# Activation transposes moved from TensorE to VectorE blocks and DMA, with a reordered product schedule, in a one-core hybrid decoder layer

## The chip, the cores and the metric

One NeuronCore of a Trainium2 chip runs the whole layer in one launch. The metric is the device time of that launch in microseconds (us). Five engines work side by side: TensorE (PE in the profile, with its weight loads as PEld), VectorE (DVE), ScalarE (ACT), GpSimd (POOL) and SyncE (SP), which here issues every DMA, the transfers between HBM and SBUF or within SBUF, in program order.

## The reference

The layer takes 256 tokens of width 2048 in float32 and computes

    h = rmsnorm(x);  y = h @ w_in                       # 2048 x 5120
    mix = [differential attention(q, k, v), conv module(u)] @ w_out
    x = x + rmsnorm(mix)
    h = rmsnorm(x)                                      # the second norm
    f = (silu(h @ w_gate) * (h @ w_up)) @ w_down        # D_FF = 5632
    x = x + rmsnorm(f)

The change touches the last three lines: the feed-forward half, and the end of the norm that feeds it.

## The kernel before

Every weight is used in float32 accuracy from two reduced-precision pieces. A weight tile of 512 x 512 (1 MB) is loaded by SP into a tile `w` (three buffers), or, for some tiles, into `raw`; ACT copies it rounded into `wh` (L185, L922), DVE subtracts to get the rest `wl` (L186, L923). PE then does, for each half of the tokens (`tb`, 128 of them), 12 matmuls of 128 x 512: four with high operand times `wh`, four with low operand times `wh`, interleaved, then four with high operand times `wl`. These 12 are called a step here. `wh` and `wl` have four buffers each, so tile i+4 can be split once PE is done with tile i.

D_FF is cut into 11 columns of 512, f = 0 to 10, in four parts (0 to 2, 3 to 5, 6 to 8, 9 and 10). Column 0 is done plainly. Each other column is a `Pair`: gate and up share products of a Strassen-like scheme. Seven products P1 to P7 take one step each, the gate tiles g0, g1 and the up tiles u0, u1 two steps each; 15 steps in all with the up tiles of the column before (the `fill`) placed inside. The order is P1, u0 (of the column before, or down tiles of the part before), P7, P6, u1, P5, P2, P3, g0, g1, P4. Four subtractions of whole tiles (L956) make the weights of later products; `last_sum` is one of them. P7 goes into PSUM bank b7, the products P1, P6, P5, P3 accumulate in bank b1. After P5, ACT copies b1 to a tile `s` and DVE adds b7 (L1025, L1026); P3 cannot write b1 before that copy.

After u1, DVE forms the activation `sg` (L1014, L1035): 128 tokens by 512 columns for each tb. `act_put` turns it round for the down product: PE transposes eight 128 x 128 blocks into PSUM (L1044; L845 for column 0), ACT rounds them into the high piece of the tile `act` (L208) and DVE makes the low piece (L209).

When the columns of a part are done, the down product runs for four column groups n = 0 to 3, each over the two or three `act` tiles of the part, two steps a tile. In the last part the loads of the norm's gain `gpf` and of `xres` (3 MB together, `reload`) are queued after the split of the first down tile.

The order of work on every engine is the order of the Python program. A list of steps is walked; before each step the side jobs that are due run (`yield n` means: go on n steps later), then the split of the tile four places ahead of the one just finished, with the loads that this lets go (`pump`) and its `post` subtractions. So whatever a job issues stands in each engine's queue ahead of what later steps issue. `needs` makes a down step wait in the program for its `act_put`.

`residual(1)` ends the first half for the second 128 tokens: transposes, then the sums of H2 tiles for the scheme (`form_sums`, `split_sums`), four squares (ACT), and the norm factor `rffn` that the first gate waits for.

Pools that matter here: T has 13 tiles of 1 MB, M has three of 512 KB.

Of the kernel before, what the change touches and what calls it, by code (L numbers as in the profile page):

```python
# [31 lines left out]
P = 128  # L32
# [12 lines left out]
C = 512  # L45
# [15 lines left out]
def hybrid_layer_kernel(ctx: ExitStack, tc: tile.TileContext, x, xt, pack, lamv,  # L61
# [635 lines left out]
    def square_into(src, acc):  # L697
        j = M("junk")
        nc.scalar.activation(j[:, :C], src, ACTF.Square, accum_out=acc)
# [26 lines left out]
    def form_sums():  # L726

        r = v3(T("sums"), 4)
        h, l = H2.part(1)
        for tb in range(2):  # L730
            tok = slice(tb * P, (tb + 1) * P)

            nc.vector.tensor_tensor(out=r[:, 2 * tb:2 * tb + 2].rearrange("p a (k t) -> p (a k) t", k=4),
                                    in0=h[:, :, tok].bitcast(F32), in1=l[:, :, tok].bitcast(F32),
                                    op=ALU.add)
        for o, a, b, op in [(3, 2, 3, ALU.add), (2, 0, 2, ALU.subtract), (0, 3, 0, ALU.subtract),
                            (1, 1, 0, ALU.subtract)]:
            nc.vector.tensor_tensor(out=r[:, o], in0=r[:, a], in1=r[:, b], op=op)
        return r
# [7 lines left out]
    def residual(tb, bank):  # L747
        xr, mg = st_["x", tb], st_["mixg", tb]
        tok = slice(tb * P, (tb + 1) * P)
        square_into(bank, part[:, tb, 3:4])  # L750
        if tb:
            yield 1
        nc.vector.tensor_tensor(out=mg[:, 3 * C:], in0=bank, in1=st_["gpost"][:, 3 * C:],
                                op=ALU.mult)
        r = partial_rstd(part, tb, "rpost")

        def x2(n):
            c = slice(n * C, (n + 1) * C)
            nc.vector.scalar_tensor_tensor(out=xr[:, c], in0=mg[:, c], scalar=r[:, 0:1],
                                           in1=xr[:, c], op0=ALU.mult, op1=ALU.add)  # L760

        def tr(n):
            bk = aux_bank("ht")
            for j in range(4):
                nc.tensor.transpose(bk[:, j * P:(j + 1) * P],
                                    xr[:, n * C + j * P:n * C + (j + 1) * P], ident)
            for eng in range(2):
                for j in range(4):
                    k = n * 4 + j
                    g = pk[:, PK_GFFN + k:PK_GFFN + k + 1]  # L770
                    h, l = H2.at(k, 1, tok)
                    b = bk[:, j * P:(j + 1) * P]
                    if eng == 0:
                        nc.scalar.activation(h[:, 0], b, ACTF.Copy, scale=g)
                    else:
                        nc.vector.scalar_tensor_tensor(out=l[:, 0], in0=b, scalar=g,
                                                       in1=h[:, 0].bitcast(F32), op0=ALU.mult,
                                                       op1=ALU.subtract)

        x2(0)  # L780
        yield 1
        x2(1)
        x2(2)
        yield 1
        x2(3)
        tr(0)
        for n in range(1, 4):
            yield 1
            tr(n)
        if tb:  # L790
            yield 1
            r = form_sums()
            yield 1
            split_sums(r)
        else:
            yield 3
        for n in range(4):
            square_into(xr[:, n * C:(n + 1) * C], part2[:, tb, n:n + 1])
        yield 1
        rstd2[tb] = partial_rstd(part2, tb, "rffn")  # L800

        nc.sync.dma_start(xd[tb], xr)
        st_["x", tb] = None

    oc = []
    need = {0: [lambda: st_["av", 0]], 4: [lambda: st_["av", 1]],
# [26 lines left out]
    def post_up(f, A, k, bank):  # L833
        while ("gate", f) not in st_:
            yield 1
        sg = st_["sg", f]
        for tb in range(2):
            nc.vector.scalar_tensor_tensor(out=sg[:, tb], in0=bank[tb], scalar=rstd2[tb][:, 0:1],
                                           in1=sg[:, tb], op0=ALU.mult, op1=ALU.mult)
            dve[0] += 0.6  # L840
        yield 2
        for tb in range(2):
            bk = aux_bank("ft")
            for j in range(4):
                nc.tensor.transpose(bk[:, j * P:(j + 1) * P], sg[:, tb, j * P:(j + 1) * P], ident)  # L845
            A.put_psum(k, 4, slice(tb * P, (tb + 1) * P), v3(bk, 4))

    def down_evac(pi, last, n, tb, bank):
        c = slice(n * C, (n + 1) * C)
# [39 lines left out]
    class Act:  # L889
# [9 lines left out]
            t = self.t[f]  # L899
            return t[:, 0, k % 4:k % 4 + n, tok], t[:, 1, k % 4:k % 4 + n, tok]  # L900

        put_psum = Operand.put_psum

    class Slot:

# [22 lines left out]
    class Pair:  # L928
# [5 lines left out]
        def __init__(self, f, A, k, last):  # L934
            self.f, self.A, self.k, self.last = f, A, k, last
            cols = [(f * C, C)]
            gt = [WTile(w_gate, 4 * i * P, SPLIT, cols) for i in range(4)]
            ut = [WTile(w_up, 4 * i * P, SPLIT, cols) for i in range(4)]
            self.g, self.u = gt[:2], ut[:2]
            self.r11, self.r21, self.r12, self.r22 = gt[2], gt[3], ut[2], ut[3]  # L940
            self.x = Slot()
            p = self.p = {
                1: Product(self, 1, self.r11, None, [("w", self.r11)]),
                7: Product(self, 7, self.r12, "r", [("r", self.r12), ("r", self.r22)]),
                6: Product(self, 6, self.x),
                5: Product(self, 5, self.r11, "w", [("w", self.x)]),
                2: Product(self, 2, self.r21, None, [("r", self.r21)]),
                3: Product(self, 3, self.r22, "r"),
                4: Product(self, 4, self.x, "w")}

            p[1].post = [lambda: self.sub(self.r11, self.r12, self.r11)]
            p[7].post = [lambda: self.sub(self.x, self.r22, self.r11)]
            p[3].post = [self.last_sum]

        def sub(self, out, a, b):
            nc.vector.tensor_tensor(out=out.w, in0=a.w, in1=b.w, op=ALU.subtract)  # L956
# [5 lines left out]
        def steps(self, fill):  # L962

            fill[0][0][1].post = [lambda: self.sub(self.r12, self.r22, self.r12)]
            s = {n: [(self, t, n, 0)] for n, t in self.p.items()}
            g = [[(self, t, f"g{i}", tb) for tb in range(2)] for i, t in enumerate(self.g)]
            return (s[1] + fill[0] + s[7] + s[6] + fill[1] + s[5] + s[2] + s[3] + g[0] + g[1] + s[4])

        def up_steps(self):
            return [[(self, t, f"u{i}", tb) for tb in range(2)] for i, t in enumerate(self.u)]  # L970
# [46 lines left out]
        def after(self, what, tb):  # L1017
            if what == 1:
                self.v = v3(M("v"), 2)
                nc.scalar.copy(self.v[:, 0], self.b1)  # L1020
            elif what == 6:
                nc.scalar.copy(self.v[:, 1], self.b1)
            elif what == 5:
                self.s = M("s")[:, :C]
                nc.scalar.copy(self.s, self.b1)  # L1025
                nc.vector.tensor_tensor(out=self.s, in0=self.b7, in1=self.s, op=ALU.add)  # L1026
            elif what == "g1" and tb == 0:
                self.sg = v3(M("sg"), 2)
                spawn(self.gate(0, self.b2, self.v[:, 0])).run()
            elif what == 4:  # L1030
                spawn(self.gate(1, self.b7, self.v[:, 1])).run()
            elif what == "u1" and tb == 0:
                self.up(0, self.b1)
            elif what == "u1":
                nc.vector.tensor_tensor(out=self.s, in0=self.b8, in1=self.s, op=ALU.add)  # L1035
                self.up(1, self.s)
                st_["act", self.f] = spawn(act_put(self.A, self.k, self.sg),
                                             1 if self.last else 3)

    def act_put(A, k, sg):  # L1040
        for tb in range(2):
            bk = aux_bank("ft")
            for j in range(4):
                nc.tensor.transpose(bk[:, j * P:(j + 1) * P], sg[:, tb, j * P:(j + 1) * P], ident)  # L1044
            A.put_psum(k, 4, slice(tb * P, (tb + 1) * P), v3(bk, 4))
        yield 1

    def reload():
        load_gain(1, "gpf")
# [6 lines left out]
    for pi, (f0, f1) in enumerate(parts):  # L1056
# [25 lines left out]
        for n in range(4):  # L1082
            c = Chunk("down", A, needs=needs)
            ts = w_tiles(w_down, f0 * C, [(n * C, C)], 0, nk)
            if last and n == 0:
                ts[0][1].post.append(reload)
            if last and n == 3:
                c.done = lambda tb, c=c, pi=pi: spawn(finish(pi, tb, c.bank[tb]))
                add(c, ts, stagger=True)
                continue  # L1090
            both(lambda bank, pi=pi, last=last, n=n: post_down(pi, last, n, bank))(c)
            st = steps_of(c, ts)
            if n == 3:
                put(st[:-4])
                fill = [st[-4:-2], st[-2:]]
            else:
                put(st)
# [82 lines left out]
```

## Time and profile before

| what | us |
|---|---|
| median of 3 runs | 1071.24 (1070.83 to 1071.37) |
| the profiled execution | 1072.81 |
| its span, first to last instruction | 1071.0 |
| PE busy in it | 1049.2 |
| DVE busy | 822.8 |
| ACT busy | 562.0 |

The mean granted TensorE clock is 0.997 of full speed. The span is 1.8 us shorter than the profiled execution's time, which also holds the launch around it. A busy PE in this profile includes the pipeline's own overlap, so the spacing of matmul starts says more than the busy share.

### The profile page before, as it was taken

To read this page: it belongs to the slowest core of one execution; us is meant where nothing else is said; L and a number is where in the kernel's file an instruction comes from. 1 tells how busy PE (TensorE), PEld (TensorE's weight loads), DVE (VectorE), ACT (ScalarE), POOL (GpSimd) and SP (SyncE) were. 2 spreads that over 40 slices of the span, in tenths; PEclk is the share of its full clock that TensorE was granted. 3 is DMA by queue.
4 is the path that set the end of the run, shared out by engine and by line. 5 is a ranking of instruction groups with operands and counts; after the bars stand their busy time and mean duration, and the time that the engine had idled before them with its cause. 6 is when DMAs were issued, how large, how long until landed. Compare 5 with 4: busy or idle time off the path is not lost.

```text
span 1071.0 us, 12013 instructions
## 1 busy us (share of the span) xinstructions
PE 1049.2 (98%) x4766; PEld 863.2 (81%) x4766; DVE 822.8 (77%) x858; ACT 562.0 (52%) x586; POOL 10.8 (1%) x16
## 2 busy tenths in 40 slices
PE   9999999999999989999999999999999999999996
PEld 7778788787888768878888887888888788888885
DVE  6589989898655779875568988557898865788765
ACT  6764664665644656564354756334465643446541
POOL 0000000001000000000000000000000000000000
PEclk9999999999999999999999999999999999999999
DMA  9876555545656638276454636854653776272852
GB/s 307 290 272 204 175 180 169 185 135 180 239 198 234 198 113 305 88 269 243 156 196 158 242 121 232 294 171 129 225 184 131 242 283 220 79 277 79 317 193 79
DMA packets 114264, 213.97 MB, mean 200 GB/s; under 512 B 4088, under 2 KB 23840, under 8 KB 112928
## 3 DMA queue, kind: packets, MB, share of 16 engines
q1 hardware_dynamic: 114208, 213.21, 58.2%
q8 instruction: 37, 0.61, 0.2%
q14 instruction: 19, 0.16, 0.0%
HBM read 208.99 MB, written 4.21 MB: 199 GB/s over the span
## 4 chain that ended last, share of the span: by engine, by line
PE 83%; DVE 6%; ACT 4%; DMA 3%; issue 2%; SPq 1%; POOL 1%; DVEq 0%; POOLq 0%; ACTq 0%
PE b L1001 23%; PE mm L259 15%; PE mm L260 14%; PE mm L262 14%; PE b L1004 12%; DMA w<-in_w_in_dram 3%; DVE wl L186 2%; ACT wh L185 2%; DVE wl L923 1%; PE ft L1044 1%; DVE w L956 1%; DVE conv_acc L442 1%; DMA rb<-in_rel_bias_dram 1%; ACT wh L922 1%; PE scmm L262 1%
## 5 line engine op out<-in xcount | busy, mean ns | idle before, releaser
L186 DVE TENSOR_TENSOR wl<-w,wh 128x2048 fp32r<-128x2048 f32 (+1 forms) x160 | 340.3, 2128 | 129.4 <-ACT wh L185 129.2
L185 ACT CAST wh<-w 128x2048 fp32r<-128x2048 f32 (+1 forms) x160 | 284.8, 1782 | 179.6 <-PE mm L260 85.4
L1001 PE MATMUL b<-wh,h2h 128*128 128x512 f32 x440 | 171.9, 391 | 1.0 <-ACT sg L830 1.0
L1004 PE MATMUL b<-wh,h2l 128*128 128x512 f32 x440 | 171.3, 389 | 0.0
L259 PE MATMUL mm<-wh,act 128*128 128x512 f32 x352 | 137.3, 390 | 0.0
L260 PE MATMUL mm<-wh,act 128*128 128x512 f32 x352 | 137.0, 389 | 0.0
L259 PE MATMUL mm<-wh,xh 128*128 128x512 f32 x320 | 127.6, 399 | 1.6 <-ACT wh L185 1.6
L260 PE MATMUL mm<-wh,xl 128*128 128x512 f32 x320 | 124.8, 390 | 0.0
L923 DVE TENSOR_TENSOR wl<-w,wh 128x2048 fp32r<-128x2048 f32 x40 | 91.6, 2289 | 40.3 <-ACT wh L922 36.6
L1001 PE MATMUL b<-wl,h2h 128*128 128x512 f32 x440 | 117.7, 389 | 0.0
L922 ACT CAST wh<-w 128x2048 fp32r<-128x2048 f32 x40 | 76.4, 1911 | 74.7 <-DVE w L956 42.6
L1001 PEld LDWEIGHTS b<-wh,h2h 128*128 128x128 f32 x440 | 82.6, 188 | 18.4 <-ACT sg L830 1.4
L1001 PEld LDWEIGHTS b<-wl,h2h 128*128 128x128 f32 x440 | 82.6, 188 | 17.3
L1004 PEld LDWEIGHTS b<-wh,h2l 128*128 128x128 f32 x440 | 82.6, 188 | 17.0
L442 DVE SCALAR_TENSOR_TENSOR conv_acc<-conv_in,pk,conv_acc 128x255 f32<-128x255 f32 (+14 forms) x240 | 94.2, 462 | 0.0
L262 PE MATMUL mm<-wl,act 128*128 128x512 f32 x352 | 94.1, 389 | 0.0
L262 PE MATMUL mm<-wl,xh 128*128 128x512 f32 x320 | 87.3, 390 | 0.2 <-DVE wl L186 0.2
L923 DVE TENSOR_TENSOR wl<-raw,wh 128x2048 fp32r<-128x2048 f32 x30 | 68.1, 2288 | 22.5 <-ACT wh L922 22.5
L922 ACT CAST wh<-raw 128x2048 fp32r<-128x2048 f32 x30 | 57.4, 1914 | 48.6 <-DVE raw L956 39.9
L262 PEld LDWEIGHTS mm<-wl,act 128*128 128x128 f32 x352 | 66.1, 188 | 13.8
L260 PEld LDWEIGHTS mm<-wh,act 128*128 128x128 f32 x352 | 66.1, 188 | 13.6
L259 PEld LDWEIGHTS mm<-wh,act 128*128 128x128 f32 x352 | 66.1, 188 | 13.6
(170 smaller groups left out, 1290.6 us busy)
## 6 DMA issues: line engine op xcount, KB each, us to landing
w<-in_w_down_dram SPq DMA_DIRECT2D x44, 1024.0 KB, 5.0
w<-in_w_gate_dram SPq DMA_DIRECT2D x34, 1024.0 KB, 5.3
w<-in_w_in_dram SPq DMA_DIRECT2D x24, 1024.0 KB, 5.1
w<-in_w_up_dram SPq DMA_DIRECT2D x24, 1024.0 KB, 5.3
raw<-in_w_up_dram SPq DMA_DIRECT2D x20, 1024.0 KB, 8.7
w<-in_w_out_dram SPq DMA_DIRECT2D x16, 1024.0 KB, 5.0
w<-in_w_in_dram SPq DMA_DIRECT2D x24, 512.0 KB, 5.0
raw<-in_w_gate_dram SPq DMA_DIRECT2D x10, 1024.0 KB, 8.7
```

The source lines that it names most:

```text
L185: nc.scalar.copy(self.h[:, a:b], self.w[:, a:b])
L186: nc.vector.tensor_tensor(out=self.l[:, a:b], in0=self.w[:, a:b], in1=self.h[:, a:b].bitcast(F32), op=ALU.subtract)
L259: nc.tensor.matmul(bank, lhsT=h, rhs=t.h[:, j], start=first, stop=False)
L260: nc.tensor.matmul(bank, lhsT=l, rhs=t.h[:, j], start=False, stop=False)
L262: nc.tensor.matmul(bank, lhsT=h, rhs=t.l[:, j], start=False, stop=last)
L442: return lambda: nc.vector.scalar_tensor_tensor(out=conv_acc[:, cb, s:], in0=conv_in[:, cb, :S - s], scalar=w, in1=conv_acc[:, cb, s:], op ...
L922: nc.scalar.copy(self.h, w)
L923: nc.vector.tensor_tensor(out=self.l, in0=w, in1=self.h.bitcast(F32), op=ALU.subtract)
L956: nc.vector.tensor_tensor(out=out.w, in0=a.w, in1=b.w, op=ALU.subtract)
L1001: nc.tensor.matmul(bank, lhsT=h[:, j], rhs=rhs, start=start and pas == 0 and j == 0, stop=stop and pas == 1 and j == SPLIT - 1, skip_group ...
L1004: nc.tensor.matmul(bank, lhsT=l[:, j], rhs=rhs, start=False, stop=False, skip_group_check=True)
L1044: nc.tensor.transpose(bk[:, j * P:(j + 1) * P], sg[:, tb, j * P:(j + 1) * P], ident)
```

## The change

Four edits are made together.

1. `act_put` no longer uses PE. DVE transposes 32 x 32 blocks, one instruction of 128 x 512 for each tb, into the first half of a T tile `sgt`; 16 DMAs of 32 KB (32 partitions, rows of 512 bytes) move the blocks into its second half; `Act.put` then rounds and subtracts from there (ACT, DVE). For the last column of a part the two halves are M tiles. The DMAs are issued two steps after the transposes (one for a part's last column), the rounding five steps later (three).
2. b7 is copied to `s` by ACT after P7, and DVE adds b1 to it after P5. One tile `s` is kept for a part, its halves alternate.
3. In a pair g0 goes before P3, and `last_sum` follows the split of g0. In the down product the last tiles of n = 0 and n = 1 are done after both groups' other tiles.
4. In `residual(1)` the squares come one step earlier and ahead of the sums, and `split_sums` comes after the norm factor.

```diff
-        if tb:
-            yield 1
-            r = form_sums()
-            yield 1
-            split_sums(r)
-        else:
-            yield 3
+        yield 1 if tb else 3
         for n in range(4):
             square_into(xr[:, n * C:(n + 1) * C], part2[:, tb, n:n + 1])
+        if tb:
+            r = form_sums()
         yield 1
         rstd2[tb] = partial_rstd(part2, tb, "rffn")
...
+        if tb:
+            split_sums(r)
...
-            p[3].post = [self.last_sum]
+            self.g[0].post = [self.last_sum]
...
-            return (s[1] + fill[0] + s[7] + s[6] + fill[1] + s[5] + s[2] + s[3] + g[0] + g[1] + s[4])
+            return (s[1] + fill[0] + s[7] + s[6] + fill[1] + s[5] + s[2] + g[0] + s[3] + g[1] + s[4])
...
+            elif what == 7:
+                if self.A not in st_:
+                    st_[self.A] = M("s")
+                self.s = v3(st_[self.A], 2)[:, self.f % 2]
+                nc.scalar.copy(self.s, self.b7)
...
             elif what == 5:
-                self.s = M("s")[:, :C]
-                nc.scalar.copy(self.s, self.b1)
-                nc.vector.tensor_tensor(out=self.s, in0=self.b7, in1=self.s, op=ALU.add)
+                nc.vector.tensor_tensor(out=self.s, in0=self.b1, in1=self.s, op=ALU.add)
...
-                st_["act", self.f] = spawn(act_put(self.A, self.k, self.sg),
-                                             1 if self.last else 3)
-
-    def act_put(A, k, sg):
-        for tb in range(2):
-            bk = aux_bank("ft")
-            for j in range(4):
-                nc.tensor.transpose(bk[:, j * P:(j + 1) * P], sg[:, tb, j * P:(j + 1) * P], ident)
-            A.put_psum(k, 4, slice(tb * P, (tb + 1) * P), v3(bk, 4))
-        yield 1
+                st_["act", self.f] = spawn(act_put(self.A, self.k, self.sg, self.last))
+
+    def act_put(A, k, sg, last):
+        if last:
+            m = M("sgt")
+        else:
+            t = T("sgt")
+            m, raw = t[:, :2 * C], t[:, 2 * C:]
+        for tb in range(2):
+            nc.vector.transpose(
+                out=m[:, tb * C:(tb + 1) * C].rearrange("p (u j c) -> p j u c", u=4, j=4),
+                in_=sg[:, tb].rearrange("p (j u c) -> p j u c", j=4, u=4))
+        yield 1 if last else 2
+        if last:
+            raw = M("actr")
+        src, dst = (v.rearrange("p (b q x) -> p b q x", b=2, q=4) for v in (m, raw))
+        for i in range(4):
+            for u in range(4):
+                nc.sync.dma_start(dst[u * 32:(u + 1) * 32, :, i], src[i * 32:(i + 1) * 32, :, u])
+        yield 3 if last else 5
+        A.put(k, raw)
...
-        put_psum = Operand.put_psum
+        def put(self, k, raw):
+            for tb in range(2):
+                r = raw[:, tb * C:(tb + 1) * C].rearrange("p (i k c) -> p k i c", i=4, k=4)
+                h, l = (t.rearrange("p k (i c) -> p k i c", i=4)
+                        for t in self.at(k, 4, slice(tb * P, (tb + 1) * P)))
+                nc.scalar.copy(h, r)
+                nc.vector.tensor_tensor(out=l, in0=r, in1=h.bitcast(F32), op=ALU.subtract)
...
-            if n == 3:
+            if n == 0:
+                st0 = st
+            elif n == 1:
+                put(st0[:-2] + st[:-2] + st0[-2:] + st[-2:])
+            elif n == 3:
                 put(st[:-4])
```

Column 0 (`post_up`) calls the same `act_put`.

## Rows read from the trace of the kernel before

**Rows 1.** The page's first part: busy us, share, instructions

```profile
PE 1049.2 (98%) x4766; PEld 863.2 (81%) x4766; DVE 822.8 (77%) x858; ACT 562.0 (52%) x586; POOL 10.8 (1%) x16
```

**Rows 2.** Timeline of PE in columns 2, 5, 10: start, length, line, tiles

```profile
456.99 0.50 PE L1001 MATMUL b<-wh,sumh 128*128 128x512 f32 x1 [0.78 <-ACT s L1025]
...
645.64 0.39 PE L1001 MATMUL b<-wh,h2h 128*128 128x512 f32 x1
...
647.46 1.07 PE L1001 MATMUL b<-wl,h2h 128*128 128x512 f32 x4
649.17 0.50 PE L1001 MATMUL b<-wh,sumh 128*128 128x512 f32 x1 [0.65 <-ACT s L1025]
...
652.03 1.04 PE L1044 MATMUL ft<-ident,sg 128*128 128x128 f32 x8
652.82 0.47 PE L1001 MATMUL b<-wh,h2h 128*128 128x512 f32 x1
...
989.82 0.50 PE L1001 MATMUL b<-wh,sumh 128*128 128x512 f32 x1
```

**Rows 3.** Waits of all engines: total us, times, longest us

```profile
PE b L1001 <- ACT s L1025: 2.5, 4, 0.8
```

**Rows 4.** Timeline of PE and ACT where the pairs begin

```profile
384.52 0.50 PE L1001 MATMUL b<-wh,h2h 128*128 128x512 f32 x1 [1.00 <-ACT sg L830]
...
396.83 1.90 ACT L922 CAST wh<-w 128x2048 fp32r<-128x2048 f32 x1 [4.62 <-DVE w L956]
...
399.27 0.79 PE L1001 MATMUL b<-wh,sumh 128*128 128x512 f32 x1 [3.49 <-ACT v L1020]
```

**Rows 5.** Timeline of DVE in column 5

```profile
644.12 2.28 DVE L956 TENSOR_TENSOR w<-raw,w 128x2048 f32<-128x2048 f32 x1
646.32 0.74 DVE L1014 SCALAR_TENSOR_TENSOR sg<-b,rffn,sg 128x512 f32<-128x512 f32 x1
...
648.36 2.29 DVE L186 TENSOR_TENSOR wl<-w,wh 128x2048 fp32r<-128x2048 f32 x1
```

**Rows 6.** Groups by line and shape: busy us, mean ns, idle before

```profile
L482 DVE TENSOR_SCALAR nat<-nat,mv,ln_rs 128x1024 f32<-128x1024 f32 x2 | 1.5, 813 | 0.8 <-POOL ln_rs L102 0.8
```

**Rows 7.** Timeline of ACT: the split of g0 in columns 2, 5, 10

```profile
450.63 1.92 ACT L185 CAST wh<-w 128x2048 fp32r<-128x2048 f32 x1 [1.24 <-DMA w<-in_w_gate_dram]
...
644.07 1.91 ACT L185 CAST wh<-w 128x2048 fp32r<-128x2048 f32 x1 [2.50 <-DMA w<-in_w_gate_dram]
...
983.48 1.92 ACT L185 CAST wh<-w 128x2048 fp32r<-128x2048 f32 x1 [1.26 <-PE b L1004]
```

**Rows 8.** DMA issues: KB each, median us from issue to landing

```profile
w<-in_w_down_dram SPq DMA_DIRECT2D x44, 1024.0 KB, 5.0
...
out_dram<-xres SPq DMA_DIRECT2D x8, 256.0 KB, 2.2
...
rb<-in_rel_bias_dram SPq DMA_DIRECT2D x1, 1.0 KB, 6.1
```

**Rows 9.** Timeline of SP near 52 us: start, length of the issue

```profile
52.09 0.37 SPq L165 DMA_DIRECT2D w<-in_w_in_dram  x1
...
53.52 0.51 SPq L377 DMA_DIRECT2D rb<-in_rel_bias_dram  x1
```

**Rows 10.** Windows: length, busy by engine, granted clock, DMA share, GB/s

```profile
399.20:402.80 3.60, 3.53 (x10) 2.83 (x11) 3.60 (x2) 3.60 (x4) 0.00 (x0) 0.60 0.00 0
1009.00:1023.00 14.00, 14.00 (x67) 11.68 (x66) 9.34 (x8) 5.28 (x5) 0.00 (x0) 1.00 1.00 388
```

**Rows 11.** Waits of SP's own queue: total us, times, longest us

```profile
SPq L1116 <- DMA w<-in_w_in_dram: 1.7, 4, 0.6
```

**Rows 12.** Timeline of PE: the end of u1 in column 5

```profile
676.52 1.07 PE L1001 MATMUL b<-wl,h2h 128*128 128x512 f32 x4
```

**Rows 13.** Timeline of SP: loads for the next part, and of down weights

```profile
655.68 26.03 SPq L165 DMA_DIRECT2D w<-in_w_down_dram  x7
681.75 1.05 SPq L165 DMA_DIRECT2D raw<-in_w_up_dram  x2
```

More of the change, by code (lines that the diff above doesn't have):

```diff
@@ L840, in post_up @@
             dve[0] += 0.6
-        yield 2
-        for tb in range(2):
-            bk = aux_bank("ft")
-            for j in range(4):
-                nc.tensor.transpose(bk[:, j * P:(j + 1) * P], sg[:, tb, j * P:(j + 1) * P], ident)
-            A.put_psum(k, 4, slice(tb * P, (tb + 1) * P), v3(bk, 4))
+        yield from act_put(A, k, sg, False)
     def down_evac(pi, last, n, tb, bank):
@@ L1036, in after @@
                 self.up(1, self.s)
-                st_["act", self.f] = spawn(act_put(self.A, self.k, self.sg),
-                                             1 if self.last else 3)
-    def act_put(A, k, sg):
-        for tb in range(2):
[L1042 to L1045, printed above, removed]
-        yield 1
+                st_["act", self.f] = spawn(act_put(self.A, self.k, self.sg, self.last))
[5 more added lines that the diff above has]
+            m, raw = t[:, :2 * C], t[:, 2 * C:]
+        for tb in range(2):
+            nc.vector.transpose(
[10 more added lines that the diff above has]
+        A.put(k, raw)
     def reload():
```

## Prediction

> **What bounds the kernel now.** I read the page's busy shares first: PE is busy 98% of the span, every other engine less [rows 1]. Busy time of a pipelined engine says little, so I went to the starts of its matmuls. In a step of column 5 eight matmuls take 647.46 - 645.64 = 1.82 us, 0.227 us each, and a step of 12 takes 2.72 us [rows 2]. PE keeps this spacing nearly throughout, so the end is set by the number of matmuls and by the few places where a start is late. The waits show what makes PE late in the pairs: ACT's copy to `s`, 2.5 us in four waits [rows 3]; and the timelines show two more waits where the pairs begin, 1.00 and 3.49 us [rows 4]. So the kernel is bound by PE with almost no waiting, and a change gains what it takes off PE and loses every wait that it adds. The span is 1071.0 us; the profiled execution took 1072.81, the median is 1071.24. I add the sum to the median, since only differences are in it.
>
> **The change part by part.**
>
> *Transposes off PE.* Eight transposes start at 652.03 and the next matmul at 652.82, and that one lasts 0.47 instead of 0.39 us: 0.79 + 0.08 = 0.87 us a column [rows 2]. Eleven columns: -9.6 us.
>
> *The copy of b7.* P3 should follow 4 x 0.227 = 0.91 us after 647.46, at 648.37, and starts at 649.17: 0.80 us late where the profile shows 0.65 [rows 2]. The 2.5 us become 2.5 x 0.80/0.65 = 3.1, which go, since ACT can copy b7 seven steps ahead of P3: -3.1 us.
>
> *The norm factor.* Squares and factor now precede `split_sums`, so the first gate is released earlier and the 1.00 us goes. The 3.49 us stays: it ends with the split of P6, which follows a DVE subtraction [rows 4], and DVE still has all its sums to make: -1.2 us together, 0 to -6.
>
> *VectorE's order in a pair.* This is the first cost. g0 is split before P3, and its weights are late: ACT starts on g0 at 644.07 when they land [rows 7]. In the old order DVE split P3 in that wait. Now DVE does, after ACT's 1.91: g0 2.2, `last_sum` 2.2 (644.12 to 646.32), the three activation operations 2.04 (646.32 to 648.36) [rows 5], two transposes, P3 2.2, then the addition to `s`, about 0.7. The transpose has no row. Nearest is a DVE operation of 128 x 512, 0.74 us issued in 0.67 [rows 5]; a one-input operation of 128 x 1024 takes 0.81, so 0.41 would be the least [rows 6], and twice 0.67 the most. I take 0.62, as it moves the same elements. So the addition ends 1.93 + 2.2 + 2.2 + 2.04 + 1.24 + 2.2 + 0.7 = 12.5 us after ACT starts g0: at 656.6 in column 5. P3, which may not write b1 before that, is due two g0 steps after its old place, 648.37 + 5.44 = 653.8: 2.8 us late. Column 2: 450.63 + 12.5 = 463.1 against 456.99 - 0.95 + 5.44 = 461.5, 1.6 late; column 10: 983.48 + 12.5 = 996.0 against about 995.1, 0.9 late [rows 2, 7]. Six columns (2, 4, 5, 7, 8, 10) follow another pair of their part like these; at 1.4 us each: +8.4 us, 5 to 15 with the bounds of the transpose. Columns 1, 3, 6 and 9 I leave at nothing: down tiles fill their pairs, and DVE is ahead there. What comes behind on DVE (g1, P4, and the chain to the next P6) is late too; the wait before P6 was 3.49 us once [rows 4]. I put +1.5 us on columns 2, 5 and 8: +4.5, 0 to 10.
>
> The Trainium skill ("VectorE: DVE Perf Modes", the three transpose paths) gives 311 ns for a 128 x 128 block transposed in 32 x 32 pieces, and advises TensorE for a full transpose. Four make 1.24 us an instruction by that page, an estimate; with it the six columns would lose 6 x 2 x 0.6 = 7 us more. No row here shows the operation.
>
> *The sixteen DMAs.* The second cost, and the larger. Three facts come from rows. Issuing costs SP 0.37 to 0.51 us each [rows 9]: sixteen take 16 x 0.42 = 6.7 us. Landing: 256 KB alone take 2.2 us, 1 MB takes 5.0 [rows 8]; but the 1 KB of `rb` took 6.1 us [rows 8], issued 1.4 us after a 1 MB load [rows 9]. So a small transfer waits for what SP issued before it. A busy queue moves 388 GB/s, 2.7 us per MB [rows 10]. And SP waits at L1116 for landings of weights that it doesn't touch [rows 11]; I read a limit of about eight in flight. So the second eight go only as the first land, and the last lands 8 x 0.42 + 2.2 = 5.6 us after the first. Without the limit it would be 2 us less.
>
> Columns 2, 5, 8. Let T be the end of u1, 677.43 in column 5 (676.52 + 0.91) [rows 12]. SP's order after it is one down load, two raw loads for the next part, then the sixteen. The raw loads were issued at 681.75, T + 4.3 [rows 13]. Three loads take 5.0 + 2 x 2.7 us: nothing small lands before about T + 14.3, the last of the sixteen at T + 19.9, and `put` adds about 1.3 us (the first ACT and DVE operations of 128 x 512; DVE's issued in 0.67 [rows 5], ACT's taken as about the same). Due is T + 8 x 2.72 = T + 21.8. That would just do, but for the DMAs of the column before. Those stand in SP's queue ahead of the first down load, which was issued at 655.68 [rows 13]. By the chain above, P4 is split at 661.0; column 4's DMAs go from 659 to about 667 and the load lands about 672. DVE's operations behind its split (two more down splits, then the activation) are then about 5 us late, and with them everything to the arrival: T + 26.2, 4.4 us late. +13.2 us for three, 0 to 25.
>
> Column 10. The same lag, but due is only T + 4 x 2.72 = T + 10.9, and `reload` has put 3 MB more ahead. From about T - 1.5 on seven loads are queued before the sixteen (a down tile, `gpf`, two of `xres`, three more down tiles): 2.3 + 7 x 2.7 = 21.2 us, the 2.3 being 5.0 - 2.7, to T + 19.7; with 5.6 and 1.3 more, T + 26.6: 15.7 us late. If `reload` came as early as before, three loads would be left and it would be 8 late, my lower end; with dearer issues 18.
>
> *The clock.* After the 3.49 us wait the window that follows shows a granted clock of 0.60, that is half speed (1.2 GHz) for most of it; 0.4 x 3.6 = 1.4 us lost [rows 10]. Waits of 1 us show no such fall. Four waits of 4 us or more: 4 x 1.5 = +6, 1.5 to 8.
>
> *Nothing.* The extra DMA volume is 5.8 MB, 15 us of queue time over the run, inside a queue that is half idle. Evacuations of n = 0 and n = 1 come later but before their banks are wanted. ACT keeps its number of copies.
>
> **Sum.** -9.6 - 3.1 - 1.2 + 8.4 + 4.5 + 13.2 + 15.7 + 6 = +33.9. 1071.2 + 33.9 = **1105 us**. Least loss by the lower ends: -9.6 - 3.1 - 6 + 5 + 0 + 0 + 8 + 1.5 = -4; most: -9.6 - 3.1 + 15 + 10 + 25 + 18 + 8 = +63.
>
> **The rivals.**
>
> *The blocks arrive in time (faster).* The steps between transposes and `put` (8.2 us for the DMAs of a last column, more elsewhere) cover the transfers. For it: DVE and DMA are not full, and small transfers alone land in 2.2 us [rows 8]. Against it: `rb`'s 6.1 us. It decides at the last landing: before T + 9.6 in column 10 and T + 20.5 in columns 2, 5 and 8. Then -13.9 + 8.4 or less on P3: 1058 to 1066 us, about 1062. Chance 0.11.
>
> *Only the last column is late.* DVE catches up in the down products, where it has slack, so that columns 2, 5 and 8 arrive in time as in my first reckoning; column 10 loses 8 to 10 and the clock 1.5: -13.9 + 8.4 + 9 + 1.5 = +5 to +12, 1076 to 1083. Chance 0.19, of which 0.04 within 0.2% of 1071.
>
> *VectorE is the bound.* Transposes at the upper end and issues of 0.5 us: P3's wait grows by 1.4 us in six columns (+8), each arrival by 16 x 0.1 plus the added lag (+2.5 in four), P6's by 1: +22 on mine, 1127. Chance 0.15.
>
> *My sum*, 1088 to 1118: 0.55.
>
> A measurement here can tell 0.2% (2 us) from no change. Faster 0.11, same 0.04, slower 0.85. The range leaves out the faster rival and the far half of the dear one: 1074 to 1124.
>
> **What would show it.** Right: no L1044; PE waits before the third down tile of columns 2, 5, 8 and, longest, before the second of column 10, ended by `act`; ACT's rounding of `act` waits for a DMA there; waits before P3 ended by DVE's addition to `s`; granted clock at half after the long ones. Wrong: the sixteen land within 6 us behind queued loads, so that PE never waits for `act`; or DVE's transpose well over 1.3 us; or a wait in columns 1, 3, 6, 9 that I left out.

## The result, and the profile after

The changed kernel takes 1139.7 us (median of four runs, 1137.2 to 1141.6) beside 1071.3 for the kernel before in the same job: ratio 1.0637, 95% interval 1.0624 to 1.065, so 68.4 us slower. The forecast was 1105, slower by 34: the sign and the places were right, but the loss is twice the forecast one and the time lies above the stated range, 1074 to 1124. The profiled execution's span is 1137.6 us.

The page's first part, and the waits of PE (us in total, times, longest), answer to [rows 1] and [rows 3]:

```profile
PE 1059.7 (93%) x4678; PEld 867.1 (76%) x4678; DVE 836.0 (73%) x880; ACT 561.9 (49%) x586; POOL 12.8 (1%) x16
```

```profile
PE mm L259 <- ACT act L901: 44.1, 4, 16.9
PE b L1001 <- DVE sg L1008: 12.3, 3, 4.8
PE b L1001 <- ACT v L1020: 3.5, 1, 3.5
PE mm L259 <- DVE sg L1014: 2.3, 1, 2.3
PE b L1001 <- DVE s L1030: 1.4, 3, 0.5
```

PE has the 88 transposes less and spends 10 us more "busy", in matmuls at half clock. The waits for ACT's copy to `s` are gone, and so is the 1.00 us before the first gate [rows 4]; the 3.49 us of [rows 4] stands. Two large waits are new, beside two small ones. The first line is the down product waiting for `act` in columns 2, 5, 8 and 10 (8.8, 8.4, 10.0 and 16.9 us). The second is P7 in the pairs of columns 2, 5 and 8.

PE's timeline at two of them, in column 5 (start, length, line, tiles, idle before and what ended it):

```profile
648.64 0.76 PE L1001 MATMUL b<-wh,sumh 128*128 128x512 f32 x1 [4.84 <-DVE sg L1008]
...
724.55 0.79 PE L259 MATMUL mm<-wh,act 128*128 128x512 f32 x1 [8.39 <-ACT act L901]
...
730.14 0.54 PE L259 MATMUL mm<-wh,act 128*128 128x512 f32 x1
```

A step takes 2.72 us in [rows 2]; the one after the long wait takes 730.14 - 724.55 = 5.59. The window over it shows a granted clock of 0.50, the lower level (1.2 GHz), after PE had stood idle (length, busy by engine, clock, DMA share, GB/s), as [rows 10] did after the 3.49 us:

```profile
724.00:730.00 6.00, 5.45 (x12) 4.04 (x13) 4.44 (x4) 6.00 (x5) 0.00 (x0) 0.50 0.46 170
```

Where the blocks' time goes is in SP's timeline, beside [rows 9, 13]. First column 3's blocks (transposed while the pair of column 4 runs), then column 4's, column 5's and column 10's:

```profile
626.55 0.37 SPq L165 DMA_DIRECT2D w<-in_w_up_dram  x1
626.96 11.83 SPq L1063 DMA_DIRECT2D sgt<-sgt  x16
638.89 0.53 SPq L165 DMA_DIRECT2D w<-in_w_up_dram  x1
...
674.93 10.77 SPq L1063 DMA_DIRECT2D sgt<-sgt  x16
685.80 1.62 SPq L165 DMA_DIRECT2D w<-in_w_down_dram  x3
...
707.73 14.65 SPq L1063 DMA_DIRECT2D actr<-sgt  x16
...
1075.10 15.26 SPq L1063 DMA_DIRECT2D actr<-sgt  x16
```

and in the summary of their line (duration of an issue in ns, min/median/max; then us from issue to landing), with the longest of SP's waits there, which answers to [rows 11]:

```profile
L1063 SPq DMA_DIRECT2D sgt<-sgt x112: 585/595/1865, 420.6 to 1053.4; - x112
...
DMA to landing us min/median/max: 1.9/1.9/9.8
```

```profile
SPq L1063 <- DMA raw<-in_w_up_dram: 12.9, 6, 2.5
```

An issue takes SP 0.595 us, not the 0.37 to 0.51 of [rows 9], and over the eleven columns sixteen hold it for 10.8 to 15.3 us, since part of the time it waits for weights to land before it may issue the next. No weight load goes out meanwhile: the `w_up` load at 638.89 starts 12.3 us after the one at 626.55.

What that does to the other engines, in column 5, in the timelines of ACT and of DVE:

```profile
640.41 1.14 ACT L901 CAST act<-sgt 128x512 fp32r<-128x512 f32 x2 [5.32 <-DMA sgt<-sgt]
641.46 1.91 ACT L922 CAST wh<-raw 128x2048 fp32r<-128x2048 f32 x1
```

```profile
643.40 2.29 DVE L923 TENSOR_TENSOR wl<-raw,wh 128x2048 fp32r<-128x2048 f32 x1 [1.04 <-ACT wh L922]
645.61 2.29 DVE L956 TENSOR_TENSOR w<-raw,w 128x2048 f32<-128x2048 f32 x1
647.81 0.68 DVE L1008 TENSOR_TENSOR sg<-b,v 128x512 f32<-128x512 f32 x1
```

ACT comes to the rounding of column 3's blocks and stands 5.32 us for them, with a weight split (L922) behind it in its queue; DVE's split, a subtraction and the gate addition follow, and PE's P7 has waited for that addition. Over the whole run ACT waits for blocks in both kinds of column:

```profile
ACT act L901 <- DMA actr<-sgt: 69.1, 4, 20.1
...
ACT act L901 <- DMA sgt<-sgt: 37.0, 7, 5.6
```

VectorE's transposes are as cheap as forecast, 0.687 us each (line, shape, busy us, mean ns); [rows 5, 6] bounded them by 0.41 and 1.34:

```profile
L1052 DVE STREAM_TRANSPOSE sgt<-sg 128x512 f32<-128x512 f32 x22 | 14.3, 687 | 0.0
```

### The profile page after: what moved, and what is told of

It is laid out like the page before. It is cut to its first block, busy times and chain, and to the rows that moved or that the text cites. A ratio compares the mean times of both kernels' runs of the same rounds, so it can differ in the third digit from the quotient of the medians.

```text
span 1137.6 us, 12118 instructions
## 1 busy us (share of the span) xinstructions
PE 1059.7 (93%) x4678; PEld 867.1 (76%) x4678; DVE 836.0 (73%) x880; ACT 561.9 (49%) x586; POOL 12.8 (1%) x16
## 4 chain that ended last, share of the span: by engine, by line
PE 62%; DMA 14%; DVE 10%; SPq 6%; ACT 4%; issue 3%; POOL 0%; DVEq 0%; ACTq 0%; POOLq 0%
PE b L1001 15%; PE mm L259 12%; PE mm L260 12%; PE mm L262 12%; PE b L1004 8%; DVE wl L186 5%; SPq L1063 5%; DMA w<-in_w_down_dram 4%; DMA w<-in_w_up_dram 4%; DMA w<-in_w_in_dram 3%; DMA raw<-in_w_up_dram 3%; ACT wh L185 2%; DVE w L956 1%; DVE wl L923 1%; DMA actr<-sgt 1%
## 5 line engine op out<-in xcount | busy, mean ns | idle before, releaser
L185 ACT CAST wh<-w 128x2048 fp32r<-128x2048 f32 (+1 forms) x160 | 284.0, 1780 | 185.9 <-DMA w<-in_w_up_dram 42.5
L259 PE MATMUL mm<-wh,act 128*128 128x512 f32 x352 | 142.1, 404 | 46.4 <-ACT act L901 44.1
L260 PE MATMUL mm<-wh,act 128*128 128x512 f32 x352 | 141.6, 402 | 0.0
L922 ACT CAST wh<-w 128x2048 fp32r<-128x2048 f32 x40 | 76.4, 1909 | 84.8 <-DVE w L956 47.7
L259 PEld LDWEIGHTS mm<-wh,act 128*128 128x128 f32 x352 | 68.8, 195 | 62.6 <-ACT act L901 45.8
L262 PE MATMUL mm<-wl,act 128*128 128x512 f32 x352 | 96.7, 398 | 0.1
L1001 PE MATMUL b<-wh,sumh 128*128 128x512 f32 x160 | 67.3, 421 | 17.3 <-DVE sg L1008 12.3
L260 PEld LDWEIGHTS mm<-wh,act 128*128 128x128 f32 x352 | 68.6, 195 | 16.2 <-DVE act L902 1.8
```

The lines of the kernel that those rows point to most:

```text
L185: nc.scalar.copy(self.h[:, a:b], self.w[:, a:b])
L259: nc.tensor.matmul(bank, lhsT=h, rhs=t.h[:, j], start=first, stop=False)
L260: nc.tensor.matmul(bank, lhsT=l, rhs=t.h[:, j], start=False, stop=False)
L262: nc.tensor.matmul(bank, lhsT=h, rhs=t.l[:, j], start=False, stop=last)
L922: nc.scalar.copy(self.h, w)
L1001: nc.tensor.matmul(bank, lhsT=h[:, j], rhs=rhs, start=start and pas == 0 and j == 0, stop=stop and pas == 1 and j == SPLIT - 1, skip_group ...
```

## The experiments

Differences are against the median of the kernel before in the same job. The changed kernel is at +68.4.

**Edits 2 to 4 with TensorE's transposes.** `act_put`, `put_psum` and their delays are as before; the rest is as changed.

> The changed kernel with edits 2 to 4 (copy of b7, order of the products and down steps, squares earlier), but the activation transposed by TensorE as before. Theory A (the blocks' late arrival makes the whole loss; the new order costs little): the waits for act and the 12 us before P7 go with their half-clock stretches, about 67 us, and the eleven TensorE transposes come back, 11 x 0.87 = 9.6: 1139.7 - 67 = about 1070, so 1066 to 1077. Theory B (the new order costs what the prediction said, 8.4 + 4.5 us by VectorE being late before P3 and P6/P7): 1071.2 - 3.1 - 1.2 + 12.9 = 1080, so 1078 to 1090.

Measured: 1071.9 us, +0.6, ratio 1.0008 (0.9998 to 1.0017): theory A. P3 never waits. PE's waits that took the place of those removed:

```profile
PE b L995 <- DVE sg L1002: 1.8, 2, 1.0
...
PE ft L1042 <- DVE sg L836: 1.0, 1, 1.0
PE ft L1042 <- DVE sg L1008: 0.9, 2, 0.7
```

**The changed kernel without the block transfers.**

```diff
-                nc.sync.dma_start(dst[u * 32:(u + 1) * 32, :, i], ...)
...
-        A.put(k, raw)
+        A.put(k, m)
```

> The changed kernel without the 176 block transfers: the rounding reads the tile that VectorE transposed within 32 x 32 blocks, so the blocks stay where they are and the output differs from the reference; the VectorE transposes and every order are kept. Theory A (the transfers make the loss): no wait for act and none before P7, TensorE free of the transposes: 1058 to 1066. Theory B (VectorE's added work, 22 transposes of 0.69 us, and its order bound the pairs): 1075 to 1095, with waits ended by VectorE before P3 and P7.

Measured: 1079.4 us, +8.1, ratio 1.0074 (1.0059 to 1.0089). The transfers make 60 of the 68 us, but without them the kernel is still slower than before: theory A's 1058 to 1066 is missed, in B's direction. PE's waits name VectorE:

```profile
PE b L1001 <- DVE s L1030: 6.0, 6, 2.5
PE b L1001 <- DVE sg L1008: 5.8, 3, 2.5
...
PE mm L260 <- DVE act L902: 1.9, 1, 1.9
PE mm L259 <- ACT act L901: 1.3, 1, 1.3
```

**No transposing at all, edits 2 to 4.** In the first kernel the rounding reads `sg` and the transposes go:

```diff
-            for j in range(4):
-                nc.tensor.transpose(bk[:, j * P:(j + 1) * P], sg[:, tb, j * P:(j + 1) * P], ident)
-            A.put_psum(k, 4, slice(tb * P, (tb + 1) * P), v3(bk, 4))
+            A.put_psum(k, 4, slice(tb * P, (tb + 1) * P), v3(sg[:, tb], 4))
```

> The kernel with edits 2 to 4 only and no transposing at all: the rounding reads the activation as it is, so the output differs from the reference. Theory A (edits 2 to 4 cost nothing and TensorE's transposes cost 0.87 us a column; what the run without block transfers lost beyond that, 1079 against 1062, is VectorE's 22 transposes on the chain of the pairs): 1071.9 - 9.6 = 1062, so 1058 to 1066. Theory B (the loss of that run is the order g0 before P3, which TensorE's transposes only hid by giving VectorE time): 1069 to 1080, with waits ended by VectorE before P3.

Measured: 1067.4 us, -4.4, ratio 0.9964 (0.995 to 0.9977), between the theories. Taking the transposes off PE brings 5.0 us against the run with them, not 9.6:

```profile
PE b L995 <- DVE sg L1002: 6.6, 3, 3.1
...
PE b L995 <- DVE s L1024: 0.5, 1, 0.5
```

The waits before P7 grow from 1.8 to 6.6 us: PE comes there sooner and waits for VectorE's gate addition. These lines are from the slowest of the four executions (1070.16; the others took 1066.7 to 1067.6), which gained only 1.6 us on the profiled one with the transposes. It adds up so: all of PE's waits grow by 3.3 us, and the first 24 matmuls behind two of the waits before P7, at half clock, take 4.7 us more than the 2 x 2.72 = 5.44 of two steps at full clock; 9.6 - 3.3 - 4.7 = 1.6. How much of each the faster executions had is not shown.

From here to the run without transfers it is 12.5 us by the medians and 9.4 between the two profiled executions: VectorE's transposes and the later rounding. The waits before P3 rise from 0.5 to 6.0, column 10's `act` costs 3.2, and PE's waits together grow by 7.5; some 2 us of the 9.4 no wait names.

**GpSimd issues the blocks.**

```diff
-                nc.sync.dma_start(dst[u * 32:(u + 1) * 32, :, i], ...)
+                nc.gpsimd.dma_start(dst[u * 32:(u + 1) * 32, :, i], ...)
```

> The 176 block transfers issued by GpSimd, which is idle here, and not by SP; nothing else changed. Theory A (what makes the blocks late is their place in SP's program order behind weight loads that wait for a free tile, and in the queue behind the loads in flight): they start right after the transposes, some 5 to 10 us earlier, the waits for act of columns 2, 5 and 8 shrink from 9 to under 3 us each and column 10's from 17 to under 6: 1080 to 1105. Theory B (sixteen small transfers cost their issue and landing whoever issues them, and GpSimd's issue is no cheaper than SP's 0.6 us): arrivals within 3 us of the changed kernel's, 1125 to 1150.

Measured: 1092.4 us, +21.2, ratio 1.0201 (1.0184 to 1.0218): theory A. One changed issuer takes 47 of the 68 us away. GpSimd's issue is not much cheaper (its line: duration of an issue in ns), yet columns 2 and 5 no longer wait for `act`, and the two waits that are left are columns 8 and 10:

```profile
L1063 POOL DMA_DIRECT2D sgt<-sgt x112: 533/533/710, 416.0 to 1008.7; - x112
...
DMA to landing us min/median/max: 1.7/5.3/7.6
```

```profile
PE mm L259 <- ACT act L901: 12.4, 2, 9.7
```

Column 10's wait stays above the 6 us of theory A. The landing got slower by its median (5.3 us against 1.9), so it is not quicker transfers that gained the time. The blocks do start sooner: column 5's first issue comes 0.3 us behind its transposes in place of 3.7, and its last block lands 15.8 us behind them in place of 19.6. But in the run with the blocks ahead of the loads (below), still on SP, that block lands 11.5 us behind the transposes, and only 8 us are gained. So the larger part of the gain is that SP is free for the weights. GpSimd's timeline in column 10 also shows how many transfers are in flight at once: it issues eight, then waits for a landing.

```profile
1029.65 4.21 POOL L1063 DMA_DIRECT2D actr<-sgt  x8 [20.39 <-DVE sgt L1052]
1035.84 2.11 POOL L1063 DMA_DIRECT2D actr<-sgt  x4 [1.98 <-DMA actr<-sgt]
```

The Trainium skill ("Trainium Kernel Development and Optimization", Key Constraints) says that issuing from several engines saves only the sequencer's issue time, since all transfers share the same DMA engines. The trace agrees as far as it goes: by the median the blocks do not land faster from the second queue. But the issuing was no small matter here, since taking it off SP brought 47 of the 68 us.

**Eight transfers on SP.**

```diff
-                nc.sync.dma_start(dst[u * 32:(u + 1) * 32, :, i], src[i * 32:(i + 1) * 32, :, u])
+                if i % 2 == 0:
+                    w = 2 * (u // 2)
+                    nc.sync.dma_start(dst[u * 32:(u + 1) * 32, :, i:i + 2], src[i * 32:(i + 1) * 32, :, w:w + 2])
```

> The changed kernel with eight transfers of 64 KB a column in place of sixteen of 32 KB: the same bytes, queue and place, half the issues (each moves two neighbouring block columns to neighbouring places, so the blocks are partly in the wrong order and the output differs from the reference). Theory A (besides their place, the number costs: SP issues one in 0.64 us and only about eight are in flight, so that the second eight start when the first have landed): the last block lands some 5.5 us earlier in every column, the waits for act fall from 8.8, 8.4, 10.0 and 16.9 to about 3, 3, 4.5 and 11, those before P7 by a third: 1095 to 1115. Theory B (the place behind the weight loads alone decides; the number does not matter): 1130 to 1141.

Measured: 1092.9 us, +21.1, ratio 1.0193 (1.0177 to 1.0208): theory A, and better than it said. Columns 2 and 8 now wait 1.2 and 1.4 us for `act`, column 5 less; column 10 still 9.9:

```profile
PE mm L259 <- ACT act L901: 12.5, 3, 9.9
```

**Eight on SP, eight on GpSimd**: `(nc.sync if i < 2 else nc.gpsimd).dma_start(...)`.

> The changed kernel with each column's sixteen block transfers shared: SP issues eight of them, GpSimd the other eight, side by side; all blocks are moved. Theory A (it is the count on one queue: SP's time of 0.64 us for each and the limit of about eight in flight on it): like the run with eight transfers, or better, since half the blocks need not pass the loads: 1083 to 1094, with column 10's wait for act at 8 to 10. Theory B (eight transfers were quicker because they carried rows twice as long, so that the number of rows moved decides, not the issues): 1100 to 1125.

Measured: 1098.0 us, +25.9, ratio 1.0245 (1.0228 to 1.0263): between the theories. With every row moved at its old length, half the issues on SP bring 42.5 us; eight with longer rows brought 47.3. So the issues on one queue decide, and the length of the rows has at most the 5 us between. The cost is not in proportion to the count: against all sixteen on GpSimd, the first eight issues on SP cost about 5 us, the second eight 42.

**Which column's blocks.** GpSimd issues those of the seven columns that are not a part's last, `(nc.sync if last else nc.gpsimd)`, or those of the four that are, `(nc.gpsimd if last else nc.sync)`.

> The changed kernel, with GpSimd issuing the block transfers of the seven columns that are not a part's last; SP keeps those of columns 2, 5, 8 and 10. Theory A (as the prediction has it, the loss at a part's end is in large part a lag: the column before holds SP for some 10 us, and the weight loads, splits and transposes behind it come late): the waits before P7 fall to the 1.9 to 2.6 us of the run with all on GpSimd, those for act of columns 2, 5 and 8 from 9 to 3 to 5, column 10's to about 12: 1100 to 1115. Theory B (each wait for act is made by that column's own sixteen transfers on SP): only the waits before P7 shrink, 1125 to 1134.

> The counterpart: GpSimd issues the block transfers of columns 2, 5, 8 and 10, SP those of the other seven. Theory A (lag from the column before): the waits for act shrink by less than half, those before P7 stay 12 us in sum: 1112 to 1128. Theory B (each column's own transfers): the waits for act of columns 2, 5, 8 all but go, column 10's falls to 10: 1095 to 1110.

Measured: 1112.0 us, +40.5, ratio 1.0377 (1.0361 to 1.0392), and 1123.8, +52.2, ratio 1.0489 (1.0474 to 1.0505). Taking the seven away brings 28 us, the four 16; both together brought 47. Theory A: the larger part is lag handed on. The waits for `act` of the last columns, whose own blocks did not change, fall from 44.1 to 23.4 with the seven away:

```profile
PE mm L259 <- ACT act L901: 23.4, 4, 14.5
```

and only to 30.7 with the four away, where the waits before P7 stay at 12.3:

```profile
PE mm L259 <- ACT act L901: 30.7, 4, 12.0
PE b L1001 <- DVE sg L1008: 12.3, 3, 4.7
```

**Blocks ahead of the loads in the program.** The first `yield` of `act_put` goes, the second is as much longer.

> The changed kernel with the block transfers issued right behind the transposes in the program (two steps earlier, one for a part's last column; the rounding stays at its step), so that they stand in SP's queue ahead of the weight loads that followed the transposes. Theory A (place in SP's program order decides): the sixteen land within about 14 us of the transposes and not 21, the waits for act of columns 2, 5 and 8 fall from 9 to under 4: 1105 to 1128. Theory B (SP's time for sixteen issues decides, whatever their place: what stands behind them is late by as much): the waits for act shrink, but weights come late in their stead: 1132 to 1150.

Measured: 1132.9 us, +60.8, ratio 1.0569 (1.0553 to 1.0585): theory B. Columns 2, 5 and 8 no longer wait for `act` (the first line is column 10); PE waits for a weight split and for sums that are late instead:

```profile
PE mm L259 <- ACT act L901: 14.2, 1, 14.2
PE b L1001 <- DVE sg L1008: 12.5, 3, 4.4
PE b L1001 <- ACT wh L185: 12.2, 3, 4.5
PE mm L259 <- DVE fsum L849: 8.9, 2, 4.5
```

**A later rounding**: `yield 3 if last else 9`.

> One delay changed: for the columns that are not a part's last, the rounding of the moved blocks is placed nine steps behind the transfers and not five. Theory A (the 3.8, 5.0 and 3.9 us before P7 of columns 2, 5 and 8 come from ScalarE, which waits 5 us for the blocks with the next weight splits behind it in its queue): these three waits and their half-clock stretches go, 12.7 + about 6 us: 1117 to 1126. Theory B (they come from VectorE's own longer work in a pair): 1137 to 1142, the same waits.

Measured: 1141.7 us, +70.4, ratio 1.0661 (1.0645 to 1.0677): a miss for theory A, and theory B has the time but not the waits. Those before P7 fell only from 12.3 to 8.2, so ScalarE's standing was a third of them. The waits for `act` of columns 2, 5, 8 and 10 fell as well, from 44.1 to 34.4. But the rounding now came beside the first down steps, where PE waits 9.0 us for it (L902, four times) and 5.9 in column 10's part (one of the five of L901):

```profile
PE mm L259 <- ACT act L901: 40.3, 5, 10.1
PE mm L260 <- DVE act L902: 9.0, 4, 2.3
PE b L1001 <- DVE sg L1008: 8.2, 3, 3.8
```

**The reload later**: `if last and n == 2` in place of `n == 0`.

> The changed kernel with one line moved: the loads of the norm's gain and of xres, 3 MB, are queued after the split of the fifth down tile of the last part and not of the first, so behind the blocks of column 10. Theory A (column 10's blocks land behind these 3 MB, 2.7 us per MB): its wait for act falls from 16.9 to about 9: 1130 to 1135. Theory B (SP's issues and the limit on transfers in flight set that landing, or the weights of the last down tiles are late instead): 1136 to 1142.

Measured: 1135.7 us, +64.1, ratio 1.0597 (1.0579 to 1.0614), between the theories, nearer to A. Column 10's wait fell from 16.9 to 10.5 us, of which 4 us reached the end; column 2's wait, at a place that was not edited, is 2 us longer in this run.

```profile
1088.38 0.79 PE L259 MATMUL mm<-wh,act 128*128 128x512 f32 x1 [10.48 <-ACT act L901]
```

**Filling the waits with matmuls.** Ahead of the first `act` step of each part:

```diff
+        for i in range(n):    # n = 36, 35, 42, 72
+            nc.tensor.matmul(bk, lhsT=h[:, i % 4], rhs=t.h[:, i % 4], start=i == 0, stop=i == n - 1)
```

> The changed kernel with 36, 35, 42 and 72 matmuls more, into a bank that nobody reads, placed in TensorE's order where it waits for the act of columns 2, 5, 8 and 10, about as long as those waits. Theory A (the granted clock falls to half because TensorE idles there; a long wait costs its length and then some 3 us at half clock): the waits stay as long in sum, the half-clock matmuls behind them go, 4 x about 3 us: 1124 to 1131. Theory B (the half clock does not come from the idle time): 1138 to 1143.

Measured: 1137.3 us, +65.5, ratio 1.0618 (1.0603 to 1.0633): neither theory's time, and close to B's. The mean granted clock rose from 0.964 to 0.987, so the idle time does lower it. But the fillers take 185 x 0.227 = 42.0 us and 7.4 us of waiting are left:

```profile
PE mm L259 <- ACT act L916: 7.4, 4, 2.4
```

49.4 in place of 44.1: some 5 us came back as longer waits, for PE then comes sooner to the next place that the transfers set. In the changed kernel's trace the first 24 matmuls behind these four waits take 11.4 us more than 4 x 5.44 (two steps each); here it is 4.0, half of it in column 5, where 2.4 us of waiting were left and the clock fell all the same. So 7.4 us came off and 5.3 came back. The 2.9 us between the two runs are not clear of the noise (1.0603 to 1.0633 against 1.0624 to 1.065), and the stretches at half clock behind the waits before P7 were left as they are.

**Edits 2 and 4 on the kernel before.** To see whether a part of the change is worth keeping.

```diff
+            elif what == 7:
+                ...
+                nc.scalar.copy(self.s, self.b7)
...
-                nc.scalar.copy(self.s, self.b1)
-                nc.vector.tensor_tensor(out=self.s, in0=self.b7, in1=self.s, op=ALU.add)
+                nc.vector.tensor_tensor(out=self.s, in0=self.b1, in1=self.s, op=ALU.add)
```

> The kernel before with edits 2 and 4 alone (copy of b7 after P7; squares and norm factor earlier). Theory A (the waits of P3 for ScalarE's copy to s, 3.4 us of late starts, and the 1.00 us before the first gate go and nothing takes their place): 1065 to 1069. Theory B (as in the run of edits 2 to 4, waits for VectorE take their place): 1070 to 1073.

Measured: 1081.5 us, +9.7, ratio 1.0091 (1.0077 to 1.0105): worse than both theories. P3 stands one step behind P5 (P2 is between) and now waits for VectorE's addition, which stands in VectorE's queue, where only ACT's copy was waited for before:

```profile
PE b L999 <- DVE s L1027: 8.2, 6, 2.1
```

So edit 2 needs edit 3: with g0 ahead of P3 the addition is in time, and edits 2 to 4 together are worth nothing. Edit 3 by itself was not run.

**Banks of its own for P7.** In the first kernel of this section P7 takes `aux_bank("b7")`, and the transposes the two halves of one PSUM tile.

> Edits 2 to 4 with TensorE's transposes (1071.9 before), and the banks exchanged: P7 takes a PSUM bank of its own in each column, and the transposes take the pair of banks that P7's two halves shared. Theory A (P7 waits 1.0, 1.0 and 0.8 us for VectorE's gate addition, which reads the other half of the same PSUM tile; with a tile of its own it need not): these starts come on time and 2 to 3 us go: 1068 to 1070.5. Theory B (VectorE is late there anyway, so that P6, whose weights come from VectorE next, waits as long): 1071 to 1073.

Measured: 1134.0 us, +62.5, ratio 1.0581 (1.0565 to 1.0597). The waits before P7 are gone, as theory A has it, but the exchange costs far more at the transposes: the second four, into the other half of the tile, wait until DVE has read the first half.

```profile
PE ft L1041 <- DVE act L209: 49.6, 11, 6.8
```

```profile
625.92 0.60 PE L1041 MATMUL ft<-ident,sg 128*128 128x128 f32 x4
633.02 1.11 PE L1041 MATMUL ft<-ident,sg 128*128 128x128 f32 x4 [6.51 <-DVE act L209]
```

No experiment beat the kernel before with all its work done. The run with no transposing at all gains 4.4 us, so little is to be had on this road.

## Why the prediction was wrong: the right mechanism at half its size

The direction held: no transposes on PE in the pairs, waits for `act` in columns 2, 5, 8 and longest in 10, half clock after them. The size did not: 68.4 us against 33.9, more even than the +63 of all its upper ends together.

The two traces show where it went. PE's waits sum to 68.7 us in the changed kernel and 13.3 before. The first 24 matmuls behind the long waits, at half clock in part, lose 21.4 us against 1.5 (they take 7.1 to 8.8 us in place of 5.44). The transposes give 9.6 back. 55.4 + 19.9 - 9.6 = 65.7, of the 66.6 us between the spans. By steps:

- *The sixteen DMAs*, 13.2 + 15.7. This is the step that failed. The waits for `act` are 27.2 us in columns 2, 5 and 8 and 16.9 in column 10, with 2.3 more in column 10's part for a bank: column 10 was nearly right, the other three were put at half. An issue was priced at 0.42 us from loads [rows 9] and takes 0.595, and sixteen hold SP 10.8 to 15.3 us where 6.7 was written. The lag that this hands on was counted only at a part's end and as 5 us. In column 5 the transposes end 9.8 us after u1 and 2.9 in the run without transfers, a lag of 6.9; the last block lands 29.4 us after u1 where the prediction had 24.9. The transfers of the seven other columns make the larger share, 28 us of the 47 that leave with SP's queue. What the step said of the queue the runs bear out: small transfers land behind loads (up to 9.8 us in place of 1.9), about eight are in flight (which [rows 11] do not show, but GpSimd's timeline does), and the reload stands ahead of column 10 (its wait falls from 16.9 to 10.5 without it).
- *The clock*, +6 for four waits. Behind those four the trace shows 11.4 us, and 7.0 more behind the waits before P7, which had no such term. So this term was mis-sized as well. Such a stretch stands in the span as it is, but taking it away gives back less than its length: with the waits filled, 7.4 us of it went and 5.3 came back as longer waits.
- *Before P6*, +4.5 in columns 2, 5 and 8: it is P7 that waits, 5.8 us without the transfers and 12.3 with them. The place is one step off (P7 stands right ahead of P6); the engine that is late, VectorE, is right.
- *Transposes off PE*, -9.6: they went, and 5.0 us were gained by the medians where nothing stood in their place. Their removal was costed as pure gain; most of the rest came back before P7, where VectorE sets the start.
- *Copy of b7*, -3.1, and *norm factor*, -1.2: the waits named went, but edits 2 to 4 together measured +0.6. Others of about the same size (1.8, 1.0, 0.9) stand in their place.
- *VectorE's order*, +8.4 before P3: 6.0 us in six waits once the transfers are out of the way, so the mechanism and nearly the size. The size has some luck in it: the three columns that were worked out average 1.8 us, and 1.4 was booked without a reason. In the changed kernel only 1.4 us in all is left of it, as PE is late itself. The transpose's 0.62 us was right too: the starts are 0.63 apart. The Trainium skill ("VectorE: DVE Perf Modes", the three transpose paths) would have it at 1.24, an estimate from its figure for bf16 taken four times; the row shows 0.687 for the whole float32 instruction, and decides.

In two sums: everything but the transfers was forecast at -1.0 and measured +8.1; the transfers with the clock at +34.9 and measured +60.3.

The time lies beyond every case on record. The likeliest had the mechanisms that came; the dearest, VectorE as the bound with 1127, asked for transposes at their upper end, which did not come, and only its issues of 0.5 us pointed the right way. What stays open: some 2 us between the run without transposing and the one without transfers, and some 13 us that the transfers cost even on GpSimd's queue, of which column 10's wait of 9.7 and column 8's of 2.7 are the part that the trace names.

## What to carry to other kernels

Price a step that issues many small transfers by the time that it holds the issuing queue, and then ask what stands behind it there: here sixteen issues cost 11 to 15 us of weight loading each time, and columns that never waited for their blocks paid through the next ones. Work taken off the busiest engine is worth only what the next engine's lateness leaves of it; look at the shortest slack behind it before booking the whole. A stall's length and the slow clock after it both stand in the span, but where the next stall is set by a queue, taking one of them away gives back only a part.

## What the runs showed of the hardware

An issue of a 32 KB move within SBUF takes SP 0.595 us and GpSimd 0.533, against 0.37 to 0.53 for a 1 MB load. Eight transfers went out on GpSimd's queue before the ninth had to wait for a landing. A VectorE transpose of 128 x 512 float32 in 32 x 32 blocks takes 0.687 us, as long as an addition of that shape (0.68). And this program's waits hold the two halves of one PSUM tile as one: PE waited up to 6.8 us, 49.6 in eleven waits, to write a half while VectorE was still to read the other.
